# Two attention stages of a one-core encoder layer: scores two tiles at a time in a shared bank, weight splits queued behind attention, and the windowed heads issued in written order

## The chip, the cores and the metric

The kernel runs on one core of a Trainium2 chip. The metric is the device time of one execution in microseconds; three runs of the kernel before gave 1751.32 us in the median, from 1750.7 to 1754.66. The core's engines work in parallel, each through its own queue in order: TensorE (PE in the profile, its weight loads PEld), VectorE (DVE), ScalarE (ACT), GpSimd (POOL) and SyncE (SP), the last of which here only issues DMAs. PSUM is the memory that matmuls write, SBUF the one that everything else works in.

## The reference, cut to what matters

One encoder layer over a prompt of 256 tokens and a sample of 1024 tokens, model width 1024. After a norm, one projection gives the queries, keys and values of two attention branches and the logits of two gates. Branch A is a windowed attention (8 heads, 2 key heads, a sink). Branch B is a mixture over three dilations (12 heads in three groups of four), and its three outputs are merged by their log-sums. The gated sum is projected, then come an MLP and the final norm.

```
z = h @ w_in
o_a, _ = _banded_attention(qa, ka, va, A_WINDOW, 1, rel_bias[:, :A_HEADS], sink)
o_b = _dilated_mixture(qb, kb, vb, rel_bias[:, A_HEADS:])
merged = gates[:, :, 0] * (o_a.reshape(b, S, A_Q) @ w_branch_a) + gates[:, :, 1] * (o_b @ w_branch_b)
x = x + merged @ w_out
h = _rmsnorm(x, g_mlp)
return x + jnp.square(jax.nn.relu(h @ w_up)) @ w_down
```

Every attention tile does the same: scores = q k plus a bias, a row maximum, exponentials with a row sum, a transposition of the result, and a product with the values.

## The kernel before, in words

The big matmuls are made of three passes each (both operands are split into a high and a low part), and the projection works through 14 pairs of 128 columns (`PAIRS`, function `pair`) with a seven-product scheme: `seven` is 12 matmuls of 512 columns, `prompt` 24 of 256. In the middle and at the end of each of them, `pair` calls `tick` (`beside`), and every second tick, which falls on a middle, takes one step of the generator `attention_b`. This happens in the last five pairs ("mixed"), from about 355 us on. Between these calls the same function hands out steps that split the next weights: one step is a ScalarE copy that makes the high part `whi` (L316), the next a VectorE subtraction that makes the low part `wlo` (L318). `late` is true in the mixed pairs, where VectorE also forms the differences of weights (L393).

**Branch B, the dilated heads** (`attention_b`, 60 tiles, 30 steps of two tiles j and j+1). The scores of a tile are two products over 64 rows each, one a head, in two banks named `sc` (two exist); VectorE adds the bias and takes the maximum (L525), ScalarE makes the exponentials (L536) in place in `s`. Transposes go to a bank `pt` (two exist), from where ScalarE copies the tile j-2 (L271) and VectorE the tile j-1 (L273). The product with the values goes to the bank `pv`, of which one exists; it is emptied by VectorE for tile j-3 and by ScalarE for tile j-2, and GpSimd's queue sends it to DRAM. A tile is either 128 or 256 keys wide ("narrow", "wide"), or is made of two halves of 64 queries with 128 keys each ("two-piece"). In a step TensorE gets: scores j, transposes j-2, product j-3, transposes j-1, scores j+1, product j-2.

**Branch A, the windowed heads** (from L1034, 4 units of 10 tiles, 384 or 256 keys wide). Between the attention's matmuls stand those of `logits` (`fill`): five plain columns of the projection, `PLAIN`, each 48 matmuls of 512 columns and 24 of 256, handed out in eights by `mm3` (L192). `tick` spreads `fill` and the steps of `merges` (the merging of branch B, on VectorE and in small part on ScalarE) over the tiles. Up to tile 35 the order of instructions is the scheduler's; from tile 36 on it is the written one. `copy` lets ScalarE and VectorE take turns in emptying banks. From tile 36 `turn_merged` transposes the merged rows into a bank `pt` (L1188), and `low_b` subtracts (VectorE, L1200).

The block of hidden rows `h21`, which the plain columns need for their last 512 tokens, is loaded on SP's queue in `entering`, during the last pair.

Of the kernel before, what the change touches and what calls it, by code (L numbers as in the profile page):

```python
# [97 lines left out]
def encoder_kernel(  # L98
# [89 lines left out]
    def mm3(ps, pairs):  # L188

        seq = [x for (lh, ll), (rh, rl) in pairs for x in ((ll, rh), (lh, rl), (lh, rh))]  # L190
        for i, (a, b) in enumerate(seq):
            nc.tensor.matmul(ps, a, b, start=i == 0, stop=i == len(seq) - 1)  # L192
            if i % 8 == 7:
                yield
# [287 lines left out]
    def attention_b(make):  # L482


        order = [(g, i, t, tile) for i in range(2) for g in (2, 1, 0) for t, tile in enumerate(_group_tiles(g))]
# [25 lines left out]
        def scores(j):  # L511
            g, i, t, (pieces, W, c0) = order[j]
            qk, _ = held[j]
            whole, *flat = bias[g, i]
            b = whole[:, :, c0 : c0 + W] if c0 is not None else flat[pieces[0][2] >= NS]
            s = make("s", (P, 2, 2 * P), n=4)
            m = small.tile([P, 2], F32, name="m", tag="m")
            o = make("o", (P, ROW), n=6)
            for h in range(2):
                ps = bank("sc")  # L520
                rows = HALVES[h]
                for a, (p0, nq, _, _) in enumerate(pieces):
                    nc.tensor.matmul(ps[p0 : p0 + nq, :W], qk[rows, p0 : p0 + nq],  # L523
                                     qk[rows, P + P * a : P + P * a + W], start=True, stop=True)
                nc.vector.tensor_tensor_reduce(s[:, h, :W], ps[:, :W], b[:, h, :], 1.0, -3.0e38,  # L525
                                               op0=ALU.add, op1=ALU.max, accum_out=m[:, h : h + 1])
            nm, l = o[:, 2 * HD : 2 * HD + 2], o[:, 2 * HD + 2 :]
            nc.vector.tensor_scalar(nm, m, -1.0, None, op0=ALU.mult)
            live[j] = s, o
# [40 lines left out]
        for j in range(0, n + 3, 2):  # L570
# [20 lines left out]
    def entering():  # L591
# [6 lines left out]
        yield  # L598
        for i in range(2):
# [3 lines left out]
        prepare()  # L603
        yield

    unit0 = None
# [226 lines left out]
    if True:  # L833
# [104 lines left out]
        def pair(b, parts, cols, nxt, hooks, beside, late):  # L938
# [14 lines left out]
            seven(x, A11, parts[0], 0, last=False, mid=beside)  # L953
            c1 = stage("c", n=2)
            nc.scalar.activation(c1, x, AF.Copy, scale=one.scale)
            beside()
            steps_of(b, 2)
            seven(y, A12, parts[0], 1, mid=beside)
            one.sum(0, 512, y, c1)
            beside()  # L960
            steps_of(b, 2)
            pa = prompt(parts[0], "mm", beside)
# [8 lines left out]
            beside()  # L971
            steps_of(b, 2)
# [11 lines left out]
            both_()  # L984
# [3 lines left out]
            seven(z, A22, parts[2], 1, False, mid=both_)  # L988
            one.sum(512, 512, z, c2)
            one.store()  # L990
            both_()
            next(hooks, None)
            seven(x, S4, parts[3], 1, False, mid=both_)
            two.direct(0, 512, x)
            both_()
            two.direct(NS, NP, prompt(parts[3], "mm", both_))
# [28 lines left out]

    narrows.append(narrow.enter_context(tc.tile_pool(name="narrows", bufs=N_Q)))
    merged = {}
    if True:
# [13 lines left out]
        def scores(u, t):  # L1042
            st, bias = units[u]
            lo, W, c0 = tiles[t]
            s = a3("s")
            m = small.tile([P, 2], F32, name="m", tag="m")
            nm, l = nm_a[:, 2 * u : 2 * u + 2, t], l_a[:, 2 * u : 2 * u + 2, t]
# [9 lines left out]
            nc.vector.scalar_tensor_tensor(nm, m, -1.0, nsink[:, 2 * u : 2 * u + 2], op0=ALU.mult, op1=ALU.min)  # L1057
            for h in range(2):
# [792 lines left out]
```

## Time and profile before

The profiled execution took 1750.72 us; its span is 1748.9 us, so 1.8 us lie around the span. All stretches below are on the span's clock.

| stretch, us | what runs | length, us | TensorE idle, us |
|---|---|---|---|
| 355.6 to 546.0 | mixed pairs with branch B | 190.4 | 2.25 |
| 546.0 to 574.4 | rest of the last pair | 28.4 | 0 |
| 574.4 to 704.5 | branch A, tiles 0 to 35 | 130.1 | 0 |
| 704.5 to 738.9 | branch A, tiles 36 to 39 and its end | 34.4 | 3.93 |
| whole span | | 1748.9 | 32.3 |

How to read it: "idle" counts only gaps that the trace shows as such; a matmul that starts late behind a shorter gap is not in it. The lines of the trace give the start of an instruction or of a run of equal ones, how long it took until the last of them ended, engine, source line, operation, output and inputs, tile shapes and count; in square brackets stands the idle time before and who ended it. Matmuls are pipelined, so what one costs is the distance from its start to the next start. Products of plain 32-bit inputs appear twice in the trace for each one in the program.

### The profile page before, as it was taken

How to read it: one execution, taken by the hardware profiler on the slowest of the kernel's cores; microseconds unless marked ns; L12 is line 12 of the kernel's file. 1: busy time of each engine (PE TensorE's matmuls, PEld its weight loads, DVE VectorE, ACT ScalarE, POOL GpSimd, SP SyncE). 2: the span in 40 equal slices, each digit the busy share in tenths (PEclk: the TensorE clock that was granted, in tenths of full speed). 3: DMA queues.
4: the chain of work that ended last, by engine and by line, in shares of the span. 5: the costliest groups of instructions: out<-in, count | busy, mean ns of one | idle time of the engine just before them, and what ended most of it. 6: DMA issues, size and time to landing. Idle time of an engine off the chain costs nothing.

```text
span 1748.9 us, 25201 instructions
## 1 busy us (share of the span) xinstructions
PE 1716.6 (98%) x9248; PEld 1455.9 (83%) x9248; DVE 976.7 (56%) x1703; ACT 720.4 (41%) x1531; POOL 518.9 (30%) x452
## 2 busy tenths in 40 slices
PE   7999999999999999999999999999999999999998
PEld 6898888877778999888888788888888788888886
DVE  6732323455553577476548645454546776657575
ACT  6232223355553455464346443333333333333344
POOL 0212222222221464100000256555555441304040
PEclk9999999999999999999999999999999999999999
DMA  6414344566556943275212243344336844633333
GB/s 235 143 43 153 98 134 120 144 183 168 165 159 164 276 129 95 84 262 216 80 49 97 85 154 116 115 154 154 122 117 240 297 166 149 218 114 115 115 114 121
DMA packets 214781, 256.36 MB, mean 147 GB/s; under 512 B 24888, under 2 KB 144524, under 8 KB 214529
## 3 DMA queue, kind: packets, MB, share of 16 engines
q1 hardware_dynamic: 201424, 228.26, 40.4%
q0 software_dynamic: 12144, 24.38, 4.7%
q10 hardware_dynamic: 1088, 2.10, 0.3%
q8 instruction: 73, 1.20, 0.3%
q14 instruction: 52, 0.42, 0.1%
HBM read 169.10 MB, written 90.73 MB: 149 GB/s over the span
## 4 chain that ended last, share of the span: by engine, by line
PE 90%; DVE 4%; ACT 2%; issue 2%; DMA 1%; POOL 1%; SPq 0%; DVEq 0%; ACTq 0%; POOLq 0%
PE dn L351 20%; PE x L351 17%; PE mm L192 14%; PE z L351 8%; PE v L723 5%; PE pv L351 5%; PE mm L351 4%; PE y L351 4%; PE pv L1088 2%; PE pv L560 2%; PE sc L523 2%; PE pt L546 1%; PE pt L1074 1%; PE sc L1051 1%; PE tr L342 1%
## 5 line engine op out<-in xcount | busy, mean ns | idle before, releaser
L351 PE MATMUL dn<-dhi,ulo 128*128 128x512 f32 x448 | 174.6, 390 | 2.6 <-DVE ulo L186 2.6
L351 PE MATMUL dn<-dlo,uhi 128*128 128x512 f32 x448 | 174.3, 389 | 0.0
L351 PE MATMUL dn<-dhi,uhi 128*128 128x512 f32 x448 | 174.3, 389 | 0.0
L351 PE MATMUL x<-chi,wlo 128*128 128x512 f32 x424 | 167.1, 394 | 2.1 <-DVE u L1724 1.4
L351 PE MATMUL x<-clo,whi 128*128 128x512 f32 x424 | 165.6, 391 | 0.1
L351 PE MATMUL x<-chi,whi 128*128 128x512 f32 x424 | 165.1, 389 | 0.0
L318 DVE TENSOR_TENSOR wlo<-ta,whi 128x1024 fp32r<-128x1024 f32 x30 | 55.7, 1858 | 189.8 <-ACT whi L316 189.8
L318 DVE TENSOR_TENSOR wlo<-raw,whi 128x1024 fp32r<-128x1024 f32 x60 | 89.8, 1497 | 105.7 <-ACT whi L316 105.7
L393 POOL TENSOR_TENSOR tb<-raw 128x512 f32<-128x512 f32 x25 | 33.6, 1343 | 356.3 <-PE mm L192 133.8
L351 PEld LDWEIGHTS dn<-dhi,ulo 128*128 128x128 f32 x448 | 84.1, 188 | 21.2 <-DVE ulo L186 3.7
L186 DVE TENSOR_TENSOR ulo<-uraw,uhi 128x1024 fp32r<-128x1024 f32 x56 | 93.4, 1687 | 11.7 <-ACT uhi L185 11.7
L351 PEld LDWEIGHTS dn<-dhi,uhi 128*128 128x128 f32 x448 | 84.1, 188 | 17.5
L351 PEld LDWEIGHTS dn<-dlo,uhi 128*128 128x128 f32 x448 | 84.1, 188 | 17.3
L351 PEld LDWEIGHTS x<-chi,wlo 128*128 128x128 f32 x424 | 79.8, 188 | 18.3 <-issue 1.8
L351 PEld LDWEIGHTS x<-chi,whi 128*128 128x128 f32 x424 | 79.6, 188 | 17.1
L351 PEld LDWEIGHTS x<-clo,whi 128*128 128x128 f32 x424 | 79.8, 188 | 14.8 <-DVE clo L318 0.4
L1549 POOL TENSOR_TENSOR t<-raw,t 128x1024 f32<-128x1024 f32 x16 | 45.8, 2879 | 143.3 <-DMA raw<-in_w_down_dram 139.1
L1700 DVE TENSOR_TENSOR v<-v,dn 128x512 f32<-128x512 f32 x90 | 59.5, 682 | 42.5 <-PE dn L351 37.9
L1796 POOL TENSOR_TENSOR u<-u,u 128x640 f32<-128x640 f32 x16 | 25.6, 1597 | 165.5 <-ACT u L1721 165.5
L351 PE MATMUL pv<-phi,wlo 128*128 128x256 f32 x256 | 72.5, 283 | 1.7 <-ACT u L1720 1.7
L351 PE MATMUL dn<-dhi,up 128*128 128x512 f32 x224 | 73.5, 389 | 0.0
L351 PE MATMUL pv<-plo,whi 128*128 128x256 f32 x256 | 72.5, 283 | 0.0
(340 smaller groups left out, 4784.6 us busy)
## 6 DMA issues: line engine op xcount, KB each, us to landing
scr_u<-u SPq DMA_DIRECT2D x112, 320.0 KB, 2.6
uraw<-scr_u SPq DMA_DIRECT2D x56, 512.0 KB, 4.4
raw<-in_w_in_dram SPq DMA_DIRECT2D x33, 512.0 KB, 5.7
raw<-in_w_up_dram SPq DMA_DIRECT2D x32, 512.0 KB, 5.4
raw<-in_w_down_dram SPq DMA_DIRECT2D x28, 512.0 KB, 7.0
sg<-scr_g SPq DMA_DIRECT2D x32, 256.0 KB, 4.9
uraw<-scr_u SPq DMA_DIRECT2D x28, 256.0 KB, 4.6
v<-scr_v SPq DMA_DIRECT2D x96, 64.0 KB, 2.2
```

The lines of the kernel that those rows point to most:

```text
L186: nc.vector.tensor_tensor(lo, src, hi.bitcast(F32), op=ALU.subtract)
L192: nc.tensor.matmul(ps, a, b, start=i == 0, stop=i == len(seq) - 1)
L318: nc.vector.tensor_tensor(lo, src, hi.bitcast(F32), op=ALU.subtract)
L351: nc.tensor.matmul(ps, a, b, start=first and i == 0, stop=last and i == len(seq) - 1, skip_group_check=True)
L393: (nc.vector if vector else nc.gpsimd).tensor_tensor(o, x, y, op=ALU.subtract)
L523: nc.tensor.matmul(ps[p0 : p0 + nq, :W], qk[rows, p0 : p0 + nq], qk[rows, P + P * a : P + P * a + W], start=True, stop=True)
L560: nc.tensor.matmul(pv[p0 : p0 + nq, HD * h : HD * h + HD], pt[:, 2 * k + h, p0 : p0 + nq], v[:, a + k, HALVES[h]], start=k == 0, stop=k == ...
L723: nc.tensor.matmul(ps[:, :n], a, b, start=k == 0 and j == 0, stop=k == KC - 1 and j == 2)
L1088: nc.tensor.matmul(pv[:, HD * h : HD * h + HD], pt[:, 2 * b + h, :], src, start=b == 0, stop=b == W // P - 1)
L1549: nc.gpsimd.tensor_tensor(o, a, b, op=ALU.subtract)
L1700: nc.vector.tensor_tensor(v, v, ps, op=ALU.add)
L1796: nc.gpsimd.tensor_tensor(u[S1], u21, u22, op=ALU.add)
```

## The change

It has four parts. First, `scores` of branch B takes two tiles: the matmuls of tile j and of tile j+1 stand one after the other, side by side in the two halves of the same two `sc` banks, and then come VectorE's reductions of both. The step becomes: scores j and j+1, transposes j-2 (ScalarE copies), product j-3 (now ScalarE empties it), exponentials j and j+1, transposes j-1 (VectorE), product j-2 (now VectorE empties it).

Second, in the mixed pairs the steps that split the next weights are handed out two at a time in the middles, right behind the attention's step, and no longer at the ends.

Third, branch A is in written order as a whole, two tiles a step, with its own functions for scores and exponentials; four `s` tiles instead of three, three `o` tiles instead of four. ScalarE empties the first bank of transposes of every tile and the logits, VectorE the second bank and all products with values. `fill` gives 12 matmuls a step in three pieces. `turn_merged` uses a bank `mm` in this stage. Eight matmuls of `fill` stand ahead of the first tile, where 48 of 512 and 256 columns stood. The splits of the plain columns' weights (`prepare`) come at the end of each column's second block.

Fourth, `load_h21` moves from the last pair to the start of branch A.

```
     def scores(j):
+        banks = [bank("sc") for _ in range(2)]
+        at = lambda k, h: banks[h][:, 2 * P * (k - j) : 2 * P * (k - j) + order[k][3][1]]
+        for k in (j, j + 1):
+            ...
+            for h in range(2):
+                ...
+                    nc.tensor.matmul(at(k, h)[p0 : p0 + nq, :], qk[rows, p0 : p0 + nq],
+                                     qk[rows, P + P * a : P + P * a + W], start=True, stop=True,
+                                     skip_group_check=True)
+        for k in (j, j + 1):
+            ...
+                nc.vector.tensor_tensor_reduce(s[:, h, :W], at(k, h), b[:, h, :], 1.0, -3.0e38,
+                                               op0=ALU.add, op1=ALU.max, accum_out=m[:, h : h + 1])
...
             if 0 < j <= n:
                 transposes(j - 2, nc.scalar)
+            values_of(j - 3, nc.scalar)
             if j < n:
                 exponentials(j)
-            values_of(j - 3, nc.vector)
+                exponentials(j + 1)
             if 0 < j <= n:
                 transposes(j - 1, nc.vector)
-            if j < n:
-                scores(j + 1)
-            values_of(j - 2, nc.scalar)
-            if j < n:
-                exponentials(j + 1)
+            values_of(j - 2, nc.vector)
...
-            def both_(n=1):
+            def halfway(gen=None):
                 beside()
                 if late:
-                    steps_of(nb, n)
+                    steps_of(gen or nb, 2)
...
+        for j in range(0, n + 2, 2):
+            if j < n:
+                scores(*order[j])
+                next(fill)
+                if j > 2:
+                    next(merges, None)
+                next(fill)
+                for h in range(2):
+                    exponential(*order[j], h)
+                scores(*order[j + 1])
+                next(fill)
+                if j >= n - 4:
+                    turn_merged(j - n + 4, "mm")
+            if j:
+                transposes(*order[j - 2])
+            if j < n:
+                exponential(*order[j + 1], 0)
+            if j > 2:
+                values_of(*order[j - 3])
+            if j:
+                transposes(*order[j - 1])
+            if j < n:
+                exponential(*order[j + 1], 1)
+            ...
+            if j:
+                values_of(*order[j - 2])
+                if j > 2:
+                    next(merges, None)
```

On TensorE, in branch B, in a step whose first tile is wide and whose second is two-piece (L523 and L522 are scores, L546 and L553 transposes, L560 and L567 products with values, L351 the projection). Before:

```order
L351 MATMUL x<-hhi,whi 128x512
L523 MATMUL sc<-qk 128x256 x2
L546 MATMUL pt<-ident,s 128x128 x4
L560 MATMUL pv<-v,pt 64x64 x4
L546 MATMUL pt<-ident,s 128x128 x2
L523 MATMUL sc<-qk 64x128 x4
L560 MATMUL pv<-v,pt 128x64 x4
L351 MATMUL x<-hhi,wlo 128x512
```

And in the changed kernel:

```order
L351 MATMUL x<-hhi,whi 128x512
L522 MATMUL sc<-qk 128x256 x2
L522 MATMUL sc<-qk 64x128 x4
L553 MATMUL pt<-ident,s 128x128 x4
L567 MATMUL pv<-v,pt 64x64 x4
L553 MATMUL pt<-ident,s 128x128 x2
L567 MATMUL pv<-v,pt 128x64 x4
```

The second scores moved ahead of everything else, so that between the two products only the second tile's transposes are left.

On ScalarE, for two such steps (L271 copies out of banks, L536 and L543 are exponentials, L316 the split of weights, L955 and L966 an evacuation of the projection). Before:

```order
L271 ACTIVATE pt<-pt 128x512
L536 ACTIVATE s,o<-s,o 128x256 x2
L271 ACTIVATE o<-pv 128x128
L536 ACTIVATE s,o<-s,o 128x128 x2
L955 ACTIVATE c<-x 128x512
L316 ACTIVATE whi<-ta 128x1024
```

And in the changed kernel:

```order
L271 ACTIVATE pt<-pt 128x512
L271 ACTIVATE o<-pv 128x128
L543 ACTIVATE s,o<-s,o 128x256 x2
L543 ACTIVATE s,o<-s,o 128x128 x2
L316 ACTIVATE whi<-ta 128x1024
L966 ACTIVATE c<-x 128x512
```

The copy of a product now stands right behind the copy of the transposes, ahead of the exponentials, and the weights' split stands ahead of the projection's evacuation.

On VectorE, in branch A of the changed kernel, in one of the four steps in which the next column's weights are split (L1063 reductions of a 384-wide tile, L1067 the negated maximum, L1170 and L1175 parts of `merge`, L235 the weights' low part, L273 and L1101 copies of transposes and products):

```order
L1067 SCALAR_TENSOR_TENSOR nm_a<-m,nsink 128x2
L1170 TENSOR_TENSOR r<-r,e 128x3x128 x2
L235 TENSOR_TENSOR wlo<-raw,whi 128x1024
L1063 ISA s,m<-sc,bias 128x384
L1063 ISA m 128x1
L1063 ISA s,m<-sc,bias 128x384
L1063 ISA m 128x1
L1067 SCALAR_TENSOR_TENSOR nm_a<-m,nsink 128x2
L273 COPY pt<-pt 128x256
L1101 COPY o<-pv 128x128
```

Here the weights' part stands ahead of the second tile's reductions, and both copies that TensorE needs stand behind them.

More of the change, by code (lines that the diff above doesn't have):

```diff
@@ L511, in scores @@
         def scores(j):
[L512 to L526, printed above, removed]
@@ L1283, in encoder_kernel @@
+        next(fill)
+        prepare()
+        next(fill)
+        values_of(*order[n - 1])
         run(merges)
         sums_a()
+        next(fill)
+        prepare()
         w_bs = [weight(0), weight(0)]
```

166 lines of the change are left out of this document (80 added, 86 removed).

## The prediction

> **What bounds the kernel now.** I read the page's busy times first, then busy times by stretch (start and end, length, busy us of TensorE, its weight loads, VectorE, ScalarE and GpSimd, the granted clock, DMA share and GB/s).
>
> ```profile
> PE 1716.6 (98%) x9248; PEld 1455.9 (83%) x9248; DVE 976.7 (56%) x1703; ACT 720.4 (41%) x1531; POOL 518.9 (30%) x452
> 355.60:546.00 190.40, 188.15 (x1306) 146.44 (x1307) 98.80 (x401) 102.16 (x336) 44.84 (x80) 1.00 0.59 165
> 574.40:704.50 130.10, 130.10 (x932) 121.73 (x931) 87.55 (x348) 67.28 (x206) 67.39 (x110) 1.00 0.55 155
> 704.50:738.90 34.40, 30.47 (x200) 27.21 (x200) 14.50 (x48) 13.33 (x43) 3.75 (x8) 0.95 0.17 54
> ```
>
> TensorE sets the end: it is busy 98% of the span, and in the three stretches that the change touches it lacks 2.25, 0 and 3.93 us. All that can be won there is this idle time, and time in which TensorE is busy at less than its pace. What can be lost is open: the other engines are half idle, but a bank that one of them empties 0.3 us too late stops TensorE. So the question is who ends last in each step; I read steps of branch B next, by the timeline of TensorE (start, duration, operation; costs are distances between starts). A narrow step, and one with a wide and a two-piece tile:
>
> ```profile
> 371.58 0.49 PE L523 MATMUL sc<-qk 64*128 64x128 f32 x4
> 372.00 0.44 PE L546 MATMUL pt<-ident,s 128*128 128x128 f32 x2
> 372.28 0.56 PE L560 MATMUL pv<-v,pt 128*128 128x64 f32 x4
> 372.67 0.39 PE L546 MATMUL pt<-ident,s 128*128 128x128 f32 x2
> 372.99 0.49 PE L523 MATMUL sc<-qk 64*128 64x128 f32 x4
> 373.41 0.66 PE L560 MATMUL pv<-v,pt 128*128 128x64 f32 x4
> 373.88 0.48 PE L351 MATMUL x<-chi,wlo 128*128 128x512 f32 x1
> ...
> 387.52 0.70 PE L523 MATMUL sc<-qk 64*128 64x256 f32 x4
> 388.16 0.66 PE L546 MATMUL pt<-ident,s 128*128 128x128 f32 x4
> 388.65 0.56 PE L560 MATMUL pv<-v,pt 128*128 128x64 f32 x4
> 389.04 0.39 PE L546 MATMUL pt<-ident,s 128*128 128x128 f32 x2
> 389.36 0.45 PE L523 MATMUL sc<-qk 64*64 64x128 f32 x8
> 389.74 1.10 PE L560 MATMUL pv<-v,pt 128*128 128x64 f32 x8
> 390.65 0.36 PE L351 MATMUL mm<-phi,wlo 128*128 128x256 f32 x1
> ```
>
> The narrow step costs 2.30 us and the other 3.13, without a gap. Between the two products stand the second transposes and the second scores, 0.71 and 0.70 us, in which the one `pv` bank is emptied.
>
> **Branch B, what goes away.** With 64-row scores next to each other there is one change of shape less in a step. Four transposes behind scores cost 0.49, two 0.28, so two are worth 0.21; the two that now precede scores cost 0.32, and a product of four behind scores costs 0.47 against 0.39 behind transposes. So a change costs about 0.11 + 0.08 = 0.19 us, and 29 steps save **5.5 us**. The narrow step would take 2.11, the other 2.94, if nothing waited.
>
> The second scores also wait for VectorE in some steps (the bracket is idle time and who ended it; the last row is from the waits of this stretch: total, times, longest):
>
> ```profile
> 365.72 0.49 PE L523 MATMUL sc<-qk 64*128 64x128 f32 x4
> 367.53 0.69 PE L523 MATMUL sc<-qk 64*128 64x128 f32 x4 [0.33 <-DVE m L525]
> 368.62 0.48 PE L351 MATMUL z<-chi,wlo 128*128 128x512 f32 x1
> ...
> PE sc L523 <- DVE m L525: 2.1, 4, 1.2
> ```
>
> This step takes 2.90 against the 2.30 of the like one above: 0.60 lost where 0.33 is shown as idle, a factor of 1.8. With it the stretch's 2.25 us of idle time are **4.1 us**. Both scores now take banks that the step before, one whole step of projection earlier, has left, so I count all of it as saved (lower bound 2.1, the idle time alone).
>
> **Branch B, what comes.** Between the two products only the second transposes are left, 0.21 us. The product j-3 is now emptied by ScalarE, behind its copy of the transposes j-2, in the same queue:
>
> ```profile
> 372.48 0.38 ACT L271 ACTIVATE pt<-pt 128x256 f32<-128x256 f32 x1 [1.59 <-PE pt L546]
> 388.91 0.60 ACT L271 ACTIVATE pt<-pt 128x512 f32<-128x512 f32 x1 [2.12 <-PE pt L546]
> 389.31 0.28 DVE L273 COPY o<-pv 128x128 f32<-128x128 f32 x1
> ...
> 984.15 0.26 ACT L1720 ACTIVATE u<-pv 128x128 f32<-128x128 f32 x1
> 984.46 0.38 PE L351 MATMUL pv<-phi,wlo 128*128 128x256 f32 x1 [0.87 <-ACT u L1720]
> 984.69 0.28 PE L351 MATMUL pv<-plo,whi 128*128 128x256 f32 x1
> ```
>
> Let P be the start of product j-3. ScalarE's wide copy starts at P+0.26 (388.91 against 388.65), ends at P+0.86; its copy of the product, taken at the 0.28 of VectorE's, ends at P+1.14; TensorE starts 0.05 later (984.41 to 984.46), P+1.19. TensorE arrives at P + 0.39 + 0.21 = P+0.60, or 0.21 later if the second tile has four transposes. The wait is 0.59 or 0.38, and the first matmul behind a wait costs 0.11 more (984.46 to 984.69 is 0.23; a 256-column matmul behind others takes 0.12). That is 0.70 or 0.49; with the two-piece cases in between I take 0.55 for the 12 steps of this kind: 6.6 us. In narrow steps the copy starts at P+0.20, takes 0.38, ends P+0.58, the product's copy P+0.86, TensorE P+0.91: 0.31 + 0.11 = 0.42, or 0.48 where it starts at P+0.26; some have four transposes and less. 0.45 x 12 = 5.3. Where product j-3 has eight matmuls (6 steps), it ends at P+1.05 or so, its copy and hand-over P+1.38, TensorE arrives at P + 0.83 + 0.21 or + 0.42: with the refill 0.45 or 0.24, of which I take 0.27, most of these steps having the longer transposes: 1.6. Together **13.4 us lost**. Bounds: nothing, if ScalarE's copies overtook; and 0.70 x 30 = 21.
>
> What else waits behind ScalarE's copy is its own exponentials; the transposes that need them come a step later, so they have over 3 us. VectorE's reductions are behind two scores instead of one. The weights' steps, 1.05 on ScalarE and 1.22 on VectorE by the like ones of branch A below, move from the ends to behind the attention's step and ahead of an evacuation of the projection, whose bank TensorE wants back a seven-product later, 12 x 0.23 = 2.8 us; if that did not cover them, each would cost up to 1.2. GpSimd's and SP's sends of `o` only get their data a little earlier or later. I cost these at nothing: VectorE is busy 98.80 of 190.40 us and ScalarE 102.16. If that cover went, the transposes of the next step would be late. The Trainium skill ("PSUM — Partial Sum Buffer", PSUM bank collisions raise a hardware error) wants PSUM guarded by bank and quadrant and not by address, which speaks against putting two tiles into one bank: the first tile's reduction then waits for the second tile's scores. By it the reductions start 0.42 to 0.64 us later, which the slack just named takes up. No run here shows it yet.
>
> **Branch A, what goes away.** The last four tiles are already in written order and stop TensorE:
>
> ```profile
> 724.65 0.41 PE L1188 MATMUL pt<-ident,merged 128*128 128x128 f32 x2 [1.91 <-DVE oblo L1200]
> 725.37 0.46 PE L192 MATMUL mm<-hhi,wlo 128*128 128x512 f32 x1
> 728.61 0.79 PE L1074 MATMUL pt<-ident,s 128*128 128x128 f32 x4
> 725.40:729.00 3.60, 3.60 (x12) 2.78 (x11) 1.27 (x7) 2.21 (x8) 0.13 (x1) 0.53 0.12 42
> ...
> 648.28 0.39 PE L192 MATMUL mm<-hhi,whi 128*128 128x512 f32 x1
> 648.51 0.39 PE L192 MATMUL mm<-hhi,wlo 128*128 128x512 f32 x1
> ```
>
> 3.93 us are idle, and behind the longest gap eight matmuls of 512 columns take 3.24 us at a granted clock of 0.53, against 8 x 0.23 = 1.84 elsewhere: 1.4 more; refills of the gaps make some 0.3. `turn_merged` moves to a bank `mm` and no longer asks for the `pt` banks in competition with the tile's own transposes, so I count all **5.6 us** as saved.
>
> The Trainium skill ("TensorE: Matmul & The Clock Gate", Part 1: The HAM clock gate) puts the loss of the full clock down to an idle window of about 3.4 us; here 1.91 us stood before it, so the trace does not agree, and by that rule the half clock would not have come and only 4.2 would be won.
>
> **Branch A, what comes.** Tiles 0 to 35 had no gap under the scheduler's order; written order can only lose there.
>
> ```profile
> 644.90 0.60 PE L1074 MATMUL pt<-ident,s 128*128 128x128 f32 x4
> 645.34 1.45 PE L1088 MATMUL pv<-va,pt 128*128 128x64 f32 x12
> 646.60 0.36 PE L1051 MATMUL sc<-kp,qp 128*128 128x256 f32 x1
> ...
> L231 ACT ACTIVATE whi<-raw 128x1024 fp32r<-128x1024 f32 x6 | 6.3, 1048 | 0.0
> L235 DVE TENSOR_TENSOR wlo<-raw,whi 128x1024 fp32r<-128x1024 f32 x6 | 7.3, 1222 | 4.9 <-ACT whi L231 4.9
> ```
>
> A product's drain is 1.45 - 1.26 = 0.19 beyond the next start, VectorE's copy 0.28, the hand-over 0.05: the `pv` bank is free 0.52 after TensorE leaves it. Four transposes take 0.44, six 0.66 in proportion. So tiles of 384 keys have 0.14 to spare, those of 256 lack 0.08, and with the refill 0.2 to 0.24: 8 of them, 1.9 us. In four steps the split of the next column's weights stands ahead of the copies: 1.05 on ScalarE, 1.22 on VectorE. Of the 2.3 at worst and nothing at best (87.55 of 130.10 us busy) I take 0.9, as the copies stand directly behind it in the step but its own step has 8 us: 3.6. At the start ten transposes stand together, 0.4. Sum **5.9 lost**, so branch A is worth +0.3; bounds +5.5 and -5.6.
>
> `load_h21` moves past the loads of the last pair on SP's queue.
>
> ```profile
> hlo<-scr_h SPq DMA_DIRECT2D x2, 512.0 KB, 9.0
> ```
>
> Issued by about 577 us and landing 9 us later, they are there at 586; the prompt-side matmuls of the first column last to about 588. Cost nothing, with 2 us to spare; the last pair's own loads have less beside them, and TensorE did not wait there.
>
> **Sum.** 13.4 - 5.5 - 4.1 + 0.3 = +4.1 us. The profiled execution took 1750.72, with a span of 1748.9; so 1754.8 for it. The median of the runs is 1751.32, 0.6 above: **1755.4 us**, 0.23% slower.
>
> **Rivals.** (1) *The copies are in time* (chance 0.16). One mechanism, at the `pv` bank: if ScalarE has its copy of the product done by P+0.55, TensorE does not stop, and the change wins 5.5 + 4.1 - 0.3 = 9.3: 1742.0. The point is a stall of about 0.32 us a step (9.3 over 29); below it the kernel is faster. For it: VectorE's copy of the same bank started at 389.31, 0.10 after the product ended. Against: the order of ScalarE's queue, with 0.38 or 0.60 ahead of the copy.
>
> (2) *Branch A pays for branch B* (0.30). The weights' splits fall into VectorE's free third and only the narrow transposes stall: +4.1 - 3.6 = +0.5, near 1752, no change. For it: VectorE's 42 free microseconds. Against: its order puts the split before the copies.
>
> (3) *Branch A's queues run late* (0.13). If the splits cost their 2.3 and `h21` lands 2 us behind its need, or two of the pauses bring the half clock (1.4 each), branch A adds 5.6 + 2 more: 1761 to 1763. For it: a pause of 1.91 did so once. Against: the new pauses are under 0.7.
>
> (4) *The change does not order what it says* (0.05): the two tiles of a step share a bank, the reductions wait for both, exponentials come so late that the next transposes wait, and the 4.1 are not saved: 1759.5. Against: 3 us of slack.
>
> My forecast holds the other 0.36.
>
> **How the numbers follow.** The likeliest case has 1752 to 1759 as its own range; with (1) partly and (3) wholly taken in, 1745 to 1763, leaving out the full gain of (1). What a measurement of this kernel can tell from no change is about 0.2%, 3.5 us: 1747.8 to 1754.8. Faster: (1) and a sixth of (2), 0.21. Slower: (3) and (4), 0.18; of my own case, whose middle lies 0.6 above that line, 0.21; of (2) 0.04: together 0.43. The same: 0.36.
>
> **What would show it.** In the changed profile: matmuls of the second product with an idle time of 0.2 to 0.6 and ScalarE's `o` as releaser in nearly all 30 steps; no waits of scores for `m`; the stretch of branch B longer by 3 to 4 us; no `oblo` releaser and no half clock in the last tiles; gaps of 0.1 to 0.9 in branch A released by VectorE's `o`. It is wrong if the products start without a gap, if the steps shrink by less than 0.19 where they do not wait, or if branch A's stretches together change by more than 3 us.

## The result and the profile after

The changed kernel took 1757.75 us in the median of 6 runs (1754.4 to 1760.77) against 1751.32 before: a ratio of 1.0034, 95% interval [1.002, 1.0048]. The profiled execution of the changed kernel was the fastest of its six, 1754.40 us with a span of 1752.6; it is 3.7 us longer than the profiled one of before, while the medians differ by 6.4. Slower runs also had a lower mean granted clock: 0.999 at 1754.40 us, 0.996 at 1760.77 us. As an estimate, 0.003 of 1757 us is 5.3 us, most of the distance between the fastest and the slowest of the six.

Busy times by stretch (start and end, length, busy us of TensorE, its weight loads, VectorE, ScalarE, GpSimd, granted clock, DMA share, GB/s). The stretches are cut at the same two matmul blocks in both kernels: the last prompt block of the last plain pair and that of the last mixed pair, then the long run of output-projection matmuls. Before:

```profile
345.64:571.51 225.87, 223.59 (x1502) 177.28 (x1500) 109.33 (x411) 112.59 (x351) 48.54 (x85) 1.00 0.62 171
571.51:788.77 217.26, 213.33 (x1397) 192.71 (x1396) 137.45 (x464) 111.75 (x313) 71.45 (x117) 0.99 0.55 167
```

And after:

```profile
345.33:576.12 230.79, 221.63 (x1501) 176.19 (x1500) 108.30 (x411) 109.36 (x351) 52.01 (x91) 1.00 0.59 164
576.12:791.46 215.34, 213.27 (x1397) 191.81 (x1396) 136.30 (x469) 119.66 (x310) 67.89 (x111) 1.00 0.56 172
```

The stretch with branch B is 4.9 us longer, the one with branch A 1.9 shorter. In branch B TensorE is busy 2.0 us less than before and idle 9.2 us, where it was idle 2.3. Who it waits for stands in the waits of TensorE in that stretch (total, times, longest):

```profile
PE sc L522 <- DMA qk<-scr_kb: 4.5, 7, 1.7
PE pv L567 <- ACT o L271: 1.9, 10, 0.3
PE pv L567 <- ACT pt L271: 1.1, 1, 1.1
```

The waits of scores for VectorE's `m` are gone and the forecast waits for ScalarE's `o` are there, but the largest item was in no part of the prediction: scores wait for the loads of queries and keys, `qk`. (The lines show only gaps; as before, the loss is larger than the gap. They make 7.5 of the 9.2 us: smaller gaps, like the 0.14 us between 381.21 and 381.35 in the narrow step below, are in none of them.)

One undisturbed narrow step on TensorE, the copies of ScalarE in it, and the first and the last three rows of a step with a wide and a two-piece tile:

```profile
379.50 0.72 PE L522 MATMUL sc<-qk 64*128 64x128 f32 x8
380.15 0.44 PE L553 MATMUL pt<-ident,s 128*128 128x128 f32 x2
380.42 0.56 PE L567 MATMUL pv<-v,pt 128*128 128x64 f32 x4
380.82 0.39 PE L553 MATMUL pt<-ident,s 128*128 128x128 f32 x2
381.35 0.66 PE L567 MATMUL pv<-v,pt 128*128 128x64 f32 x4
381.81 0.48 PE L351 MATMUL z<-hhi,wlo 128*128 128x512 f32 x1
...
380.62 0.38 ACT L271 ACTIVATE pt<-pt 128x256 f32<-128x256 f32 x1 [3.04 <-PE pt L553]
381.02 0.28 ACT L271 ACTIVATE o<-pv 128x128 f32<-128x128 f32 x1
...
496.30 1.08 PE L522 MATMUL sc<-qk 64*128 64x256 f32 x12
...
498.28 0.44 PE L553 MATMUL pt<-ident,s 128*128 128x128 f32 x2
498.88 1.10 PE L567 MATMUL pv<-v,pt 128*128 128x64 f32 x8 [0.16 <-ACT o L271]
499.79 0.48 PE L351 MATMUL x<-chi,wlo 128*128 128x512 f32 x1
```

The narrow step takes 2.31 us, as before (2.30). The eight scores cost 0.65 and not the 0.84 that the prediction added up from two times 0.42, and the second product starts 0.53 behind the transposes, which are worth 0.21: the forecast stall, at P+0.93 where P+0.91 was worked out (P is 380.42). Saving and stall cancel in this step. The other step takes 3.50 us (3.49 by these rounded starts), and there the second product starts 0.60 behind its transposes, with ScalarE's `o` as releaser. And here is what a load that comes late does, in a step of the same kernel:

```profile
373.62 0.49 PE L522 MATMUL sc<-qk 64*128 64x128 f32 x4 [1.70 <-DMA qk<-scr_kb]
374.47 0.49 PE L522 MATMUL sc<-qk 64*128 64x128 f32 x4 [0.37 <-DMA qk<-scr_kb]
```

Against the like steps without such a wait, these loads cost 2.4 us at 373.6, 1.4 at 482.4, and 0.7, 0.5 and less at four more: 5.05 us in all (the lengths of the steps and of the stretches between them, compared one by one).

### The profile page after: what moved, and what is told of

Read it like the earlier page. It is cut to its first block, busy times and chain, and to the rows that moved or that the text cites. A ratio compares the mean times of both kernels' runs of the same rounds, so it can differ in the third digit from the quotient of the medians.

```text
span 1752.6 us, 25156 instructions
## 1 busy us (share of the span) xinstructions
PE 1714.8 (98%) x9248; PEld 1453.5 (83%) x9248; DVE 973.3 (56%) x1708; ACT 725.4 (41%) x1528; POOL 520.1 (30%) x452
## 4 chain that ended last, share of the span: by engine, by line
PE 68%; DVE 3%; ACT 3%; DMA 2%; issue 1%; SPq 1%; POOL 0%; ACTq 0%; DVEq 0%
PE dn L351 20%; PE mm L192 13%; PE x L351 11%; PE z L351 5%; PE pv L351 5%; PE y L351 3%; PE pv L1098 2%; PE pv L567 2%; PE mm L351 1%; PE sc L522 1%; PE pt L1085 1%; PE pt L553 1%; DMA scr_g<-z 1%; PE sc L1061 1%; PE sc L1062 1%
## 5 line engine op out<-in xcount | busy, mean ns | idle before, releaser
L351 PE MATMUL dn<-dhi,ulo 128*128 128x512 f32 x448 | 174.6, 390 | 3.4 <-DVE ulo L186 3.4
L351 PE MATMUL dn<-dhi,uhi 128*128 128x512 f32 x448 | 174.3, 389 | 0.0
L351 PE MATMUL dn<-dlo,uhi 128*128 128x512 f32 x448 | 174.3, 389 | 0.0
L351 PE MATMUL x<-chi,wlo 128*128 128x512 f32 x424 | 167.1, 394 | 2.0 <-DVE u L1746 1.4
L351 PE MATMUL x<-clo,whi 128*128 128x512 f32 x424 | 165.7, 391 | 0.1
L351 PE MATMUL x<-chi,whi 128*128 128x512 f32 x424 | 165.2, 390 | 0.0
L318 DVE TENSOR_TENSOR wlo<-raw,whi 128x1024 fp32r<-128x1024 f32 x60 | 90.2, 1503 | 100.3 <-ACT whi L316 100.3
L351 PEld LDWEIGHTS dn<-dhi,ulo 128*128 128x128 f32 x448 | 84.1, 188 | 22.1 <-DVE ulo L186 4.7
L351 PEld LDWEIGHTS dn<-dhi,uhi 128*128 128x128 f32 x448 | 84.1, 188 | 17.5
L351 PEld LDWEIGHTS dn<-dlo,uhi 128*128 128x128 f32 x448 | 84.1, 188 | 17.2
L351 PEld LDWEIGHTS x<-chi,wlo 128*128 128x128 f32 x424 | 79.8, 188 | 18.3 <-issue 1.8
L351 PEld LDWEIGHTS x<-chi,whi 128*128 128x128 f32 x424 | 79.6, 188 | 17.1
L351 PEld LDWEIGHTS x<-clo,whi 128*128 128x128 f32 x424 | 79.8, 188 | 14.9 <-DVE clo L318 0.4
L271 ACT ACTIVATE pt<-pt 128x512 f32<-128x512 f32 (+1 forms) x70 | 39.1, 559 | 93.7 <-PE pt L553 74.4
L351 PE MATMUL pv<-phi,wlo 128*128 128x256 f32 x256 | 72.5, 283 | 1.7 <-ACT u L1742 1.7
L351 PE MATMUL dn<-dhi,up 128*128 128x512 f32 x224 | 73.5, 389 | 0.0
```

The costliest lines, as they stand in the source:

```text
L271: nc.scalar.activation(out, in_, AF.Copy)
L318: nc.vector.tensor_tensor(lo, src, hi.bitcast(F32), op=ALU.subtract)
L351: nc.tensor.matmul(ps, a, b, start=first and i == 0, stop=last and i == len(seq) - 1, skip_group_check=True)
```

## The experiments

**Where the loss is, and how steady.** The first group splits the change and repeats it. `b_only` is the kernel before with `attention_b` of the change:

```
     def scores(j):
-            for h in range(2):
-                ps = bank("sc")
+        banks = [bank("sc") for _ in range(2)]
...
+            values_of(j - 3, nc.scalar)
             if j < n:
                 exponentials(j)
-            values_of(j - 3, nc.vector)
+                exponentials(j + 1)
```

> Only the first part of the change (branch B's scores of two tiles together, the step's new order); weights' steps, branch A and the loads of h21 as before. Theory 1 (the second tile's queries and keys are needed some 1.6 us earlier in the step and arrive late): the whole loss of the change is here, branch B's stretch is 5 us longer than before's, matmuls L522 wait for loads of qk for 3 to 7 us in all, and the time is 1756 to 1759. Theory 2 (the prediction's: the single bank for products stalls each step): also about 4 us slower, but spread evenly over the 30 steps and without waits for qk. Theory 3 (the moved weights' steps delay the loads on SP's queue): then this kernel has few waits for qk and takes 1751 to 1753.

Measured: 1758.01 us (1755.7 to 1762.52), ratio 1.0036 [1.0024, 1.0048]. The two largest waits in branch B:

```profile
PE sc L522 <- DMA qk<-scr_kb: 5.3, 6, 2.2
PE pv L567 <- ACT o L271: 2.3, 11, 0.4
```

Both expected things are there: the even stalls for the bank and the waits for qk, which need no moved weights' steps. Theory 3 alone cannot explain the loss.

`a_only` is its complement, the change with `attention_b` of before:

```
     def scores(j):
-        banks = [bank("sc") for _ in range(2)]
+            for h in range(2):
+                ps = bank("sc")
...
-            values_of(j - 3, nc.scalar)
             if j < n:
                 exponentials(j)
-                exponentials(j + 1)
+            values_of(j - 3, nc.vector)
```

> The change without its first part: branch B as before, but weights' steps, branch A in written order and the late h21 loads as changed. If the loss lies in branch B alone (theories 1 and 2), 1.9 us are won in branch A and the time is 1749 to 1750. If the moved weights' steps are to blame (theory 3), waits in branch B remain and it takes 1753 to 1757.

Measured: 1754.19 us (1749.7 to 1757.81), ratio 1.0011 [1.0002, 1.0019]. That misses the 1749 to 1750. Branch A's stretch is 215.4 us, so its gain of 1.9 is there; but branch B's is 228.8 against 225.9, and its scores now wait for qk too:

```profile
PE sc L523 <- DVE m L525: 1.9, 2, 1.1
PE sc L523 <- DMA qk<-scr_kb: 1.7, 2, 1.4
PE sc L523 <- DMA qk<-scr_qb: 0.3, 1, 0.3
```

The second part of the change moves the weight loads against the loads of the steps, and that is enough to make some late even with the old order. So theory 3 holds for a part.

`after_again` is the changed kernel unaltered.

> The changed kernel once more, for how the waits for qk vary from one execution to another: time 1756 to 1759; if the loads are late by chance, its profile has these waits at other steps and with another sum than the 4.5 us of the first profile; if they are late by the order of the queue, at the same steps with the same sum.

Measured: 1756.77 us (1753.6 to 1767.26), ratio 1.0038 [1.0023, 1.0053]. The profile has 5.3 us of waits for `qk` at the same places (the first step, those at 366, 373.6 and 390, and in the second half the one at 482 to 486), with other lengths: branch B's stretch is 233.4 us here and 230.8 in the first profile. The places stay, the lengths vary, and with them the times of this kernel: its nine runs spread over 13.7 us, where the 26 runs of before in this group lie within 4.5.

A late load can also cost the clock. Here the step at 390 waits 0.86 us for `qk` (0.24 in the first profile), and from 394.38 to 398.00 us the granted clock is 0.53; in the first profile it is 1.00 in that step. In `b_only` scores wait 2.17 us at 372.87, and the clock is 0.55 up to 376 and 0.50 up to 380 us. Of the nine runs the fastest, 1753.60 us, had a mean granted clock of 0.999 and the slowest, 1767.26 us, of 0.993. As an estimate, 0.006 of 1757 us is 10.5 us, most of the spread; behind which waits the clock fell in the runs without a trace is not shown.

**Are they late because they are issued late?** `qk_early`:

```
-            qk = held[j] = [make("qk", (P, 3 * P), n=3), None]
+            qk = held[j] = [make("qk", (P, 3 * P), n=4), None]
...
-            load(j + 2)
-            load_v(j)
+            load_bias(j + 2)
             if j < n:
                 scores(j)
-            load(j + 3)
+            load(j + 4)
+            load(j + 5)
+            load_bias(j + 3)
+            load_v(j)
```

> The whole change, with four buffers for a tile's queries and keys where there were three (and five o tiles instead of six, three of the small ss tiles instead of four, to make room), and the loads of tiles j+4 and j+5 issued behind the scores of j and j+1, a step earlier than now. Theory 1: the waits of scores for qk go, branch B's stretch falls by about 5 us to that of before (190 us), the time to 1750 to 1753. Theory 2: the products' waits are unchanged and so is the time, 1756 to 1758. A rival for theory 1, that the DMA engines and not the time of issue are what is late: waits for qk stay at 2 us or more.

Measured: 1753.72 us (1750.6 to 1756.05), ratio 1.001 [1.0001, 1.0019], between the two ranges expected. Waits for qk fell to 1.0 us, but two products now wait:

```profile
PE pv L570 <- DMA v<-scr_v: 1.5, 1, 1.5
PE pv L570 <- ACT s L546: 1.2, 1, 1.2
```

The first is a load of values that this edit put behind the others; the second stands at 472 us, a step after the next such load, where ScalarE's `s` had long been ready, so I take it for the same (argued, not shown). Branch B's stretch is 227.9 us against 230.8, so 2.9 of the 5.05 us were won, and part of the wait only moved to the load that now came last.

**Is it the queue or the bytes?** `raw_act`:

```
-            nc.sync.dma_start(raw[i], cols[i])
+            (nc.scalar if vector else nc.sync).dma_start(raw[i], cols[i])
```

> The whole change with one thing moved: in the mixed pairs the two 512 KB loads of a pair's weights are issued on ScalarE's queue instead of SP's, at the same place of the program. If the loads of queries and keys are late because they stand behind these weights in one queue, the waits of scores for qk fall from 4.5 to 5.3 us to below 1.5 and the time to 1751 to 1754. If it is the 1 MB itself that takes the DMA engines, whatever its queue, the waits stay at 3 us or more and the time at 1755 to 1759.

Measured: 1756.41 us (1753.58 to 1759.6), ratio 1.003 [1.0019, 1.0042], with the same waits (5.4 us, 7 times). The weights' loads in a window of 18 us in this kernel (KB each, median us from issue to landing), and the landing times of `qk` from 366 to 376 us (least, median, most), first of `raw_act`, then of the changed kernel:

```profile
raw<-in_w_in_dram ACTq DMA_DIRECT2D x2, 512.0 KB, 5.3
DMA to landing us min/median/max: 1.9/4.5/6.6
```

```profile
DMA to landing us min/median/max: 1.7/4.6/6.4
```

The median of these eight 64 KB loads is 4.5 us, where it is 2.3 over the whole of branch B in the changed kernel: they take longer while 1 MB of weights is under way, on whichever queue, and the expectation's first half fell. But the weights are not the whole reason. In the changed kernel they are issued at 365.7, 420.0 and 474.6 us; no scores wait behind the second of these, and the waits at 357.0 and 391.7 us have no weights beside them. Ahead of 391.7 the last load of the tile is issued only at 389.69, 2.0 us before, so it is late by its issue and not by its landing. The Trainium skill ("DMA: Bandwidth & Descriptors", Queues, rings and completion order) says that each DMA engine takes turns between the queues it has work for, which would let the small loads pass; no such gain is to be seen here.

**Is the products' wait real?** If the stall at the `pv` bank is what takes back the saving, other work between the two products should free it. `between`:

```
-            if j < n:
-                scores(j)
-            load(j + 3)
             if 0 < j <= n:
                 transposes(j - 2, nc.scalar)
             values_of(j - 3, nc.scalar)
+            if j < n:
+                scores(j)
+            load(j + 3)
```

> The whole change, with one thing moved: in a step of branch B both tiles' scores stand between product j-3 and the transposes of j-1 (transposes j-2, product j-3, scores j and j+1, transposes j-1, product j-2), so that 0.65 to 1.0 us more lie between the two products. If the second product's wait for the bank is what takes back the saving of the shapes (0.40 us in a narrow step, 0.55 in a wide one with a short product, by the excess of the second transposes over 0.21 and of the product over 0.39), it goes: narrow steps fall from 2.31 to about 1.9, wide and two-piece ones from 3.50 to 2.95, in all some 10 us, and since the scores also come later, part of the waits for qk; time 1743 to 1748. Rival: the 0.53 between the products is not a wait but the price of this order of shapes; then scores in between cost their two changes of shape again, steps stay at 2.3 and 3.5 or so, and the time is 1754 to 1758.

Measured: 1752.18 us (1746.19 to 1757.45), ratio 1.0001 [0.9989, 1.0012]. The median misses the expected 1743 to 1748; the steps do not. The bank's wait is down to 0.2 us and the narrow steps take 1.99, but the waits for qk rose to 6.6 us, presumably since faster steps ask for their loads sooner. So the mechanism is shown by the steps, and its worth in time needs the loads out of the way.

`between_early` does both (against the changed kernel):

```
-            load(j + 2)
-            load_v(j)
-            if j < n:
-                scores(j)
-            load(j + 3)
+            load_bias(j + 2)
             if 0 < j <= n:
                 transposes(j - 2, nc.scalar)
             values_of(j - 3, nc.scalar)
+            if j < n:
+                scores(j)
+            load_v(j + 1)
+            load(j + 4)
+            load(j + 5)
+            load_bias(j + 3)
...
             values_of(j - 2, nc.vector)
-            load_v(j + 1)
+            load_v(j + 2)
```

> As the one before, with the loads a step earlier, now for values too: four buffers for queries and keys, those of j+4 and j+5 issued behind the scores of j and j+1, values of j+1 just ahead of these and values of j+2 at the end of the step (five o tiles, three ss tiles, to make room). If late loads cost the 5 us that the first profile shows as waits for qk, and the waits for v in the profile with early qk were these loads pushed behind, both go: no waits of scores or products for DMA, 3 to 6 us less than the run before, 1739 to 1744. Rival: the two weight loads of 512 KB each that stand in the same queue hold up whatever comes behind them; then waits of 1 to 2 us remain at the same two or three steps and under 2 us are won.

Measured: 1738.13 us (1737.44 to 1740.76), ratio 0.9928 [0.9916, 0.994], 0.9 below the range expected. The same loads that are worth 7.4 us with the scores first (`early_first`, next) are worth 14.1 here (1752.18 to 1738.13). A narrow step, and one with a wide and a two-piece tile and a product of eight matmuls ahead:

```profile
376.94 0.38 PE L556 MATMUL pt<-ident,s 128*128 128x128 f32 x2
377.16 0.56 PE L570 MATMUL pv<-v,pt 128*128 128x64 f32 x4
377.65 0.71 PE L525 MATMUL sc<-qk 64*128 64x128 f32 x8
378.29 0.44 PE L556 MATMUL pt<-ident,s 128*128 128x128 f32 x2
378.57 0.56 PE L570 MATMUL pv<-v,pt 128*128 128x64 f32 x4
378.93 0.48 PE L351 MATMUL z<-hhi,wlo 128*128 128x512 f32 x1
...
477.32 0.60 PE L556 MATMUL pt<-ident,s 128*128 128x128 f32 x4
...
479.24 0.44 PE L556 MATMUL pt<-ident,s 128*128 128x128 f32 x2
479.51 1.00 PE L570 MATMUL pv<-v,pt 128*128 128x64 f32 x8
480.33 0.48 PE L351 MATMUL z<-hhi,wlo 128*128 128x512 f32 x1
```

The narrow step takes 1.99 us instead of 2.31, the other 3.01 instead of 3.50 (the changed kernel's like step). The scores still stand between other shapes on both sides. The waits that are left in branch B:

```profile
PE pv L570 <- ACT pt L271: 0.9, 1, 0.9
PE pv L570 <- DVE o L273: 0.7, 1, 0.7
PE sc L525 <- DMA qk<-scr_qb: 0.5, 1, 0.5
PE sc L525 <- DMA qk<-scr_kb: 0.5, 1, 0.5
PE pv L570 <- ACT o L271: 0.2, 1, 0.2
```

`early_first` keeps these loads and puts the scores first again, as the change has them.

```
+            if j < n:
+                scores(j)
             if 0 < j <= n:
                 transposes(j - 2, nc.scalar)
             values_of(j - 3, nc.scalar)
-            if j < n:
-                scores(j)
```

> The whole change with its order of TensorE kept (both scores first) and only the loads of the run between_early: queries, keys and values a step earlier, four qk buffers. So it differs from between_early only in where the scores stand, and from the change only in the loads. If the products' wait for the bank costs 12 us in 29 steps, as the difference of undisturbed steps of the two profiles says, it takes 1749 to 1751, and the loads were worth 6 to 8 us of the change's 1757. If scores in between are good for more than this wait (they also give loads time), it is slower than 1752; if the wait is small and late loads were all that the change lost, it is near between_early, 1738 to 1742.

Measured: 1750.38 us (1748.29 to 1753.31), ratio 0.9994 [0.9985, 1.0002], in the range expected. Between it and `between_early` only the place of the scores differs: 12.2 us. Between it and the change only the loads differ: 7.4 us.

**The other two parts.** `between_early_ends` undoes the second part:

```
-            def halfway(gen=None):
+            def both_(n=1):
                 beside()
                 if late:
-                    steps_of(gen or nb, 2)
+                    steps_of(nb, n)
...
-            seven(z, A22, parts[2], 1, False, mid=halfway)
+            seven(z, A22, parts[2], 1, False, mid=both_)
             one.sum(512, 512, z, c2)
             one.store()
-            beside()
+            both_()
```

> As the one before, with the second part of the change undone (the steps that split weights at the ends again, one at a time). If that part is only there to take VectorE's work from in front of the reductions, its effect is gone with scores that have time, and the time is that of the run before within 2 us; if it keeps its worth of 2.7 us (the waits of scores for VectorE in the profile of before), those waits come back and it is 2 to 3 us slower; if it makes the loads late (waits for qk in the kernel without part one), it is 2 to 3 us faster.

Measured: 1736.62 us (1736.3 to 1738.46), ratio 0.992 [0.9907, 0.9933], the fastest kernel of all and within the 2 us expected; branch B's stretch is 212.7 us against 214.5. The 0.9 and 0.7 us of the list above are gone. The intervals of the two runs overlap, so the 1.5 us by which the second part costs rather than gains rest on the two profiles more than on the times.

`b_between_early` lacks branch A's part as well: the kernel before with `attention_b` of `between_early`.

```
-            load(j + 2)
-            load_v(j)
+            load_bias(j + 2)
+            if 0 < j <= n:
+                transposes(j - 2, nc.scalar)
+            values_of(j - 3, nc.scalar)
             if j < n:
                 scores(j)
-            load(j + 3)
...
+            load_v(j + 1)
+            load(j + 4)
+            load(j + 5)
...
```

> The kernel before with branch B alone replaced by that of between_early (scores between the products, early loads); weights' steps, branch A and h21 as before. Against between_early_ends it lacks only branch A and the moved h21. If these are worth the 1.9 us that the profiles show between the last prompt block of the projection and the long run of out-projection matmuls, it takes 1738 to 1739.5; if the gain there is given back later or is chance, 1736 to 1737; if branch A in written order costs something, under 1736.

Measured: 1738.94 us (1738.39 to 1739.59), ratio 0.9926 [0.9913, 0.994], in the range expected. Branch A in written order, with the late h21 loads, is worth 2.3 us by the times and, by the stretches (218.3 against 215.7), 2.6.

## Why the prediction was right, and where its sum was not

The time lies in the range, 2.3 us above the forecast, on the side forecast. The main mechanism, the stall, is there, but that the total came out is in part luck: the terms were off by more than 2.3 us and offset each other. The stall was charged 3.8 us too much, the change of shape credited 2.4 too little and branch A charged 2.2 too much; against these stand 5.9 us that the sum did not have and 1.4 that it credited too much for the scores' waits for VectorE. Without the 5.05 us of late loads the measured terms come to -2.05 us, no longer on the side forecast, and the profiled execution of `early_first` is in fact 2.3 us shorter than that of before (1748.40 against 1750.72).

The forecast for the profiled execution was +4.1 us, the measured +3.7; 3.0 of these lie in the two stretches. That the median is 6.4 us longer goes with the lower clock of the slower runs, for which the sum has no term. In the stall's own sum 0.45 x 12 is 5.4, so its parts add up to 13.6, not 13.4. In the first profile's terms, for the two stretches:

| term | predicted | measured | from |
|---|---|---|---|
| fewer changes of shape | -5.5 | -7.9 | undisturbed blocks of before against those of `between` and its like, 90.2 to 82.5, and 0.2 in the stretches |
| scores no longer wait for VectorE | -4.1 | -2.7 | steps of before, with and without the wait |
| second product waits for the bank | +13.4 | +9.6 | undisturbed blocks of the change against those of `between` and its like, 92.1 to 82.5 |
| first step's copy of transposes late | 0 | +0.85 | the step at 360.4 |
| loads of qk late | 0 | +5.05 | steps compared one by one |
| branch B | +3.8 | +4.9 | the stretch |
| branch A | +0.3 | -1.9 | the stretch |

For the first and third row I took each of the 31 blocks of branch B's matmuls behind the first, and apart from them the stretches of projection ahead of each, at the shortest among the profiles with the same order: blocks 90.2 us and stretches 91.7 for the order of before, 92.1 and 91.5 for that of the change (two blocks that are disturbed in each of its profiles put at their like ones), 82.5 and 89.1 with scores between the products. So these twelve microseconds, which the times of `early_first` and `between_early` show as 12.2, are 9.6 of wait and 2.4 in the stretches.

**The stall at the bank** was right in place and mechanism and 40% too large. ScalarE's copy of the product stands behind its copy of the transposes, and TensorE waits in nearly every step; against scores in between a narrow step loses 0.32 us (2.31 - 1.99) where 0.45 was taken, one with a wide and a two-piece tile 0.49 for 0.55, and steps of two wide tiles 0.10 to 0.32 for 0.27. With 0.65 us or more of scores in the gap it is gone.

**The change of shape** is the term that was mis-sized. "So a change costs about 0.11 + 0.08 = 0.19 us" counts what the neighbours of the scores pay, and takes the scores themselves as unchanged, twice 0.42 us. But the 0.42 held the way out to another shape: eight narrow scores in a row take 0.65. Where the second tile is two-piece, its scores gain nothing (1.01 for twelve, 0.63 + 0.38 before). Over 29 steps it is 0.27 us a step. What the runs vary is the order; that the shape sets this price, and nothing else of the neighbours, is argued and not shown apart. With scores between the products, the stretch of projection ahead of a step is 0.09 shorter besides, as it runs into transposes of its own shape (0.23 from the last projection matmul at 376.71 to the transposes at 376.94, where the change has 0.31 from 379.19 to the scores at 379.50); that is the 2.4 above.

**The loads** were left out, and that is the step that failed outright: "Both scores now take banks that the step before ... has left, so I count all of it as saved" looks at the banks only. The second tile's scores also need its queries and keys, and these they now need at the start of the step, 1.0 to 1.2 us earlier by the two steps that the prediction shows (the expectations above say 1.6, which was too much). The prediction counted SP's queue for `h21` and for the sends of `o`, not for the `qk` loads that the moved matmuls read. Without that cost the change would have been no change in time, as `early_first` shows at 0.9994 [0.9985, 1.0002].

**The first step.** ScalarE's 1.04 us of weights and a copy out of the projection stood ahead of its copy of the first transposes, and the exponentials ahead of that were late:

```profile
355.34 0.49 PE L522 MATMUL sc<-qk 64*128 64x128 f32 x4
356.95 0.49 PE L522 MATMUL sc<-qk 64*128 64x128 f32 x4 [1.12 <-DMA qk<-scr_kb]
357.48 0.29 DVE L533 CUSTOM_DVE_ANT_0 s<-sc,bias 128x128 f32<-128x128 f32 x1 [2.86 <-PE sc L522]
361.11 1.04 ACT L316 ACTIVATE whi<-raw 128x1024 fp32r<-128x1024 f32 x1
362.32 0.36 ACT L271 ACTIVATE pt<-pt 128x256 f32<-128x256 f32 x1
```

The first reduction starts at 357.48, 0.04 after the second tile's scores, though those of the first tile were there by 355.83. That is the guard by bank that the prediction drew from the Trainium skill ("PSUM — Partial Sum Buffer", PSUM bank collisions raise a hardware error), and the trace agrees with it; in all later steps the slack hides it, as said.

**Branch A** was off by 2.2 us, by what its new waits cost. The 5.6 us of the old tail were saved (no `oblo` among the releasers, a granted clock of 1.00 from 700 to 738 us). Of the 5.9 us forecast as lost, narrow tiles took 1.2 (1.9 forecast) and waits for copies of transposes 1.5, in three places (the start, and two of the four steps with a split, behind weights' parts of 1.23 us at 595.83 and 671.75), where 4.0 had been put on the splits of weights and the start:

```profile
590.32 0.44 PE L1085 MATMUL pt<-ident,s 128*128 128x128 f32 x2 [0.25 <-ACT pt L271]
598.59 0.44 PE L1085 MATMUL pt<-ident,s 128*128 128x128 f32 x2 [0.34 <-DVE pt L273]
674.51 0.44 PE L1085 MATMUL pt<-ident,s 128*128 128x128 f32 x2 [0.41 <-DVE pt L273]
755.60 0.51 PE L192 MATMUL mm<-obhi,wlo 128*128 128x512 f32 x1 [0.94 <-DVE mT L1375]
```

The last row, 1.1 us with its refill, was in no list: the first output blocks wait for VectorE. `h21` arrived in time, as forecast.

**The rivals.** (1) fell: the copies are not in time. (2) was half right, in that branch A pays, but it was the loads that decided. (3) fell in branch A, and its kind, a load behind its need, came true in branch B. (4) fell: the reductions do wait for both tiles, but no scores wait for `m`.

**The signs.** The `m` and `oblo` waits are gone, as named. ScalarE's `o` is a releaser in ten steps of the view of waits, not in nearly all, since smaller gaps such as the 0.14 above are not listed. Branch B's stretch grew by 4.9 us and not by 3 to 4. Of branch A's four gaps none was released by VectorE's `o`: three wait for copies of transposes and one for `mT`.

What stays open is how much of the lateness is the weights' doing. At 373.6 and 482 us they are the largest transfer beside the late `qk`, and moving them to another queue changed nothing, but a kernel without them was not run; at 357.0 and 391.7 they are not there. What is shown is that loads issued a step earlier are in time, but for the first step (0.9 us of waits for `qk` left in `early_first`).

## What to carry to other kernels

When matmuls move to an earlier place, list everything they read, and follow each operand back to its load, its buffer count and what else the DMA engines carry at that time; banks are only half of it. When two uses of one bank come closer together, put independent matmuls between them rather than next to them: with the loads early in both kernels, this order alone turned no change (ratio 0.9994) into 0.7% faster (0.9928). And when loads run close to their need, the spread of the runs hints at it before any trace does: 13.7 us over nine runs of the change, 3.3 over five of `between_early`.

## What the hardware showed that I had not expected

How long TensorE pauses did not alone decide whether its clock falls. In the last matmul stage, in `qk_early` (an instruction with the idle time before it, then the busy times of the stretch behind it, with the granted clock third from the end):

```profile
1387.97 0.50 PE L351 MATMUL dn<-dhi,ulo 128*128 128x512 f32 x1 [2.18 <-DVE ulo L186]
1388.00:1392.00 4.00, 4.00 (x10) 2.85 (x11) 4.00 (x7) 1.30 (x2) 0.00 (x0) 0.57 1.07 368
```

and in the changed kernel, in the same stage:

```profile
1388.94 0.50 PE L351 MATMUL dn<-dhi,ulo 128*128 128x512 f32 x1 [1.99 <-DVE ulo L186]
1388.94:1391.00 2.06, 1.66 (x6) 1.04 (x6) 2.06 (x3) 0.00 (x0) 0.00 (x0) 1.00 1.04 392
```

After 2.18 us idle the clock is 0.57, after 1.99 it is 1.00; yet the 1.91 us of the tail of before cost the clock too, and in `qk_early` a pause of 2.27 us at 754.50 did not (1.00 from 754.5 to 758.0 us). So pauses of about 2 us are enough at times, and what else decides it was not tried. The pauses of the last stage, waits for weights, also differ from profile to profile and move that stage by 1 to 2 us in kernels that are alike there.
